# Where attention's values, the normalised x and the first branch sum are prepared in a one-core encoder block

## The chip, the cores and the metric

One core of a Trainium2 chip runs the whole program. The metric is the device time of one execution in microseconds (us); three executions of the kernel before the change give 1327.68 us (median; 1327.3 to 1328.23).

## What is computed

The reference is one layer (1024 tokens, width 1024): a mixer with two branches (chunked attention with 8 heads, and a spatial gating unit, SGU), gates on both branches, an output product, then a SwiGLU feed-forward part. The lines that this change touches:

```python
xn = rmsnorm(h, norm_mix[l])
proj = xn @ w_in[l]                      # q, k, v, u, vs, gate_logits
att = chunked_rel_attention(q, k, v, att_rel_bias[l])
sgu = spatial_gating(gelu(u), gelu(vs), ...)
br_att = att @ w_br_att[l]
br_sgu = sgu @ w_br_sgu[l]
gates = sigmoid(gate_logits + b_gate[l])
merged = gates[:, :, 0] * br_att + gates[:, :, 1] * br_sgu
h = h + merged @ w_out[l]
```

## The kernel before, in words

Everything lies transposed: 128 features on the partitions, 1024 tokens along the free axis in two halves of 512. An fp32 product is made of three TensorE passes: each operand is split into a high part (a cast on ScalarE) and a low part (source minus high part, on VectorE or GpSimd), and high x high, high x low and low x high are added in PSUM. So each operand costs one ACT cast and one DVE or POOL subtraction. There is no scheduler: the order of the Python statements is the order on each engine, and each engine works through its own list in order.

The stages that matter here, in order:

- **Attention** (`scores`, `exponents`, `turn`, `values`, `put_values`, loop over 64 steps of one head and 128 queries). `put_values` writes the outputs into `att[0..3]`, one tile for each pair of heads. Behind the loop, at line 676, all four are split into `attT` (line 156 is the common `split`), half by half.
- **Attention's branch products** `bw[0, 0..7]`, 24 matmuls each (`dense`, line 195, which calls `half_unit`, line 168): 12 for the first half of the tokens, 12 for the second, each half over the four blocks of `attT`. `begin` loads and splits the weights of the next products ahead (lines 123 and 125: hi on ACT, lo on POOL).
- **SGU values** (`gate_values`): `vs` is projected, put through gelu and normalised on DVE (lines 717 and 718).
- **Mixings** (`mix_positions(g)`, four groups, placed behind `bw[0, 4]`, `bw[0, 5]` and `bw[0, 6]`): 16 small matmuls (line 754), then on DVE lines 758 and 760, then the split into `sgu` (hi on ACT, lo on POOL).
- **SGU's branch products** `bw[1, 0..7]`, again 24 matmuls each. Beside them `gate_operands` makes the right-hand sides of the gate products: it loads x again (line 820), normalises it in eight blocks `xn` (line 825, DVE, 1024 wide), splits blocks into `b11` and `b21` and differences into `t1` (line 806 casts on ACT; line 173 subtractions, by turns on DVE and POOL), and forms further differences in place (line 812, DVE). A generator is stepped once in so many matmuls, which sets the place of each of these statements.
- **Gate products** (`order_m`, `product_m`, `collect_m`, line 182 on PE): a seven-product scheme; `collect_m` adds results on DVE and multiplies gates in (line 967).

`early` holds the first gate of each branch, computed ahead; line 620 evacuates it. `branch_evac(b, 0)` multiplies a branch by it (line 792) and adds both branches (line 795, POOL). The SP queue issues all loads, in the order of the statements. The pool `late` has 6 slots; the first three weight pairs of `vs` hold them until the last `vs` product, and then `xn0..5` take them.

Of the kernel before, what the change touches and what calls it, by code (L numbers as in the profile page):

```python
# [16 lines left out]
P = 128  # L17
# [31 lines left out]
def encoder_block(ctx: ExitStack, tc: tile.TileContext, xT, w_in, w_v, w_vs, w_att, w_sgu, w_out,  # L49
# [137 lines left out]
    def late_ops(keep, n=None):  # L187

        while len(pending) > keep and n != 0:
            if next(pending[0], 0) == 0:  # L190
                pending.pop(0)
            elif n is not None:
                n -= 1

    def dense(u, rhs, evac):

# [432 lines left out]
    with tc.tile_pool(name="apool", bufs=2) as apool:  # L629
        for n in range(2):  # L630
            load_bias(n)
            fill_bias(n)
        filler = chain(project_pair(1), project_u(0), project_pair(2), project_u(1), project_pair(3),
                       project_u(2), project_u(3), dense(gw[0], xg, early_gate(0)))
        state["due"] = 0
        turning = turn_queries(0, 1)
        for i in range(len(steps) + 2):
            if i % (2 * NT) == 0 and i < len(steps):
                j = i // (2 * NT)
                if j == PAIRS - 1:  # L640
                    late_ops(0)
                att.append(slot(f"att{j}", pool=more if j in (1, 2) else slots))
            share = SHARES[j][i % 2] if i < len(steps) - 2 else (4, 4)
            if i < len(steps):
                if i % (2 * NT) == 4 and j + 1 < PAIRS:
                    load_bias(2 * j + 2)
                scores(i)
                if i % (2 * NT) == 2 * NT - 2 and j + 1 < PAIRS:
                    load_bias(2 * j + 3)
# [12 lines left out]
            if i % (2 * NT) == NT + 1 and j + 1 < PAIRS:  # L662
                turning = turn_queries(j + 1, 0)
            elif i and i % (2 * NT) == 0 and i < len(steps):
                turning = turn_queries(j, 1)
            take(turning, 1)
            split_some()
            if i >= 2:
                values(i - 2)
        put_values(len(steps) - 1)  # L670
        attT = [two_slots(f"attT{j}") for j in range(PAIRS)]
        for s in halves:
            for j in range(PAIRS):
                split([x[:, s] for x in attT[j]], att[j][:, s], nc.gpsimd if j == 2 and s is halves[0] else nc.vector)
            drain(filler)
            late_ops(0)
            state["due"] = None
            if s is halves[0]:
                split_to(units.index(bw[0, 0]) + 2)
    late = mixer.enter_context(tc.tile_pool(name="late", bufs=6))  # L680

# [102 lines left out]
    def branch_evac(b, j):  # L784
        def evac(half, s, ps):
            if j % 2 == 0:
                branch[b, half].append(slot(f"br{b}_{half}_{j}", (P, 2, HALF)))
            dst = of_branch(b, half, j)
            if j:
                nc.scalar.copy(dst, ps)  # L790
            else:
                nc.vector.tensor_tensor(out=dst, in0=ps, in1=early[b][:, s], op=OP.mult)
                if b:
                    sum_ = of_branch(0, half, 0)
                    nc.gpsimd.tensor_tensor(out=sum_, in0=sum_, in1=dst, op=OP.add)
        return evac

    right_m, xn, low_m = {}, [], []
# [1 line left out]
    def at(k, half):  # L800
        return xn[k][half] if k == KB - 1 else xn[k][:, halves[half]]
# [9 lines left out]
    def minus(dst, a, b):  # L811
        nc.vector.tensor_tensor(out=dst, in0=a, in1=b, op=OP.subtract)

    def gate_operands():


        raw, tiles = [], None
        for k in range(KB):
            raw.append(slot(f"xn{k}", pool=late if k < 6 else more))
            nc.sync.dma_start(raw[k], xT[k * P:(k + 1) * P, :])  # L820

        def norm(k, s):
            last = k == KB - 1
            dst = tmp("xn7")[:, :] if last and s == halves[1] else raw[k][:, s]
            nc.vector.scalar_tensor_tensor(dst, raw[k][:, s], g_mix[:, k:k + 1], rstd[:, s], op0=OP.mult, op1=OP.mult)
            return dst

        xn.append(norm(0, slice(0, S)))
        yield 1
        for k in range(KB):  # L830
            if k + 2 < KB:
                xn.append(norm(k + 1, slice(0, S)))
                yield 1
            elif k + 2 == KB:
                xn.append([norm(k + 1, s) for s in halves])
                yield 1
            name = "b11" if k < 4 else "b21"
            if k % 2 == 0:
                tiles = [slot(f"{name}{x}{k}", (P, 2, HALF), F32R) for x in "hl"]
            put_m(name, k, at(k, 0), tiles, k % 2, nc.gpsimd if k % 2 else nc.vector)  # L840
            yield 1
        for k in range(4):
            if k % 2 == 0:
                tiles = [slot(f"t1{x}{k}", (P, 2, HALF), F32R) for x in "hl"]
            minus(at(k, 0), at(k, 1), at(k, 0))
            put_m("t1", k, at(k, 0), tiles, k % 2, nc.gpsimd if k % 2 else nc.vector)
            yield 1
        put_low(low_m)
        for k in range(4):
            minus(at(k, 0), at(4 + k, 1), at(k, 0))  # L850
            yield 1
            if k == 3:
                t4 = tmp("t4")
                minus(t4, at(7, 0), at(k, 0))
                xn[7][0] = t4
            else:
                minus(at(4 + k, 0), at(4 + k, 0), at(k, 0))
            yield 1
            minus(at(k, 1), at(4 + k, 1), at(k, 1))
            yield 1  # L860

    def other_operands_m():

# [19 lines left out]
    for j in range(KB):  # L883
        if j == 1:
            for n, _ in enumerate(dense(gw[1], xg, early_gate(1))):
                if n % 12 == 11:
                    split_to(units.index(vsw[n // 12]) + 1)
        for n, _ in enumerate(dense(bw[0, j], attT, branch_evac(0, j))):
            if n % 4 == 3:
                next(ending, 0)  # L890
        if j == 1:
            ending = gate_values()
            next(ending)
        for g in {4: (0,), 5: (1,), 6: (2, 3)}.get(j, ()):
            mix_positions(g)
            if g == GROUPS - 1:
                ending = gate_operands()
    banks.close()
    ps_f = ctx.enter_context(tc.tile_pool(name="ps_f", bufs=6, space=PSUM))
    psum.update(wide=None, dense=[(ps_f, "dense", 6)] * 6 + [(ps_d, "dense", 2)] * 2, n=-1)  # L900
# [57 lines left out]
    def collect_m(i):  # L958
# [23 lines left out]
        elif p == "2":  # L982
# [2 lines left out]
            yield 1  # L985
            gate(0, x, x)
            yield 1
            op(nc.gpsimd, of_branch(0, 0, j), x, of_branch(0, 0, j), OP.mult)
        elif p == "6":
            e["g"] = tmp(f"gb{j}")  # L990
            op(vector, e["g"], e["c2"], e["s"], OP.add)
# [687 lines left out]
```

## Time and profile before

| | us |
|---|---|
| median of three executions | 1327.68 (1327.3 to 1328.23) |
| the profiled execution | 1328.8 |
| its span, first to last instruction | 1327.1 |
| PE busy in it | 1304.7 (98%) |
| DVE busy | 941.0 (71%) |
| ACT busy | 570.4 (43%) |
| POOL busy | 423.4 (32%) |
| mean granted TensorE clock | 0.997 of full speed |

The page gives the busy time of each engine, the span in 40 slices, and the chain of work that ended last. A timeline row reads: start, length, engine, line, operation, output<-inputs, shapes, count; in brackets, the idle time of the engine just before and what ended it. Rows of several instructions are merged (x3), and instructions of one engine overlap a little, so starts, not lengths, give the pace. A row of a waiting list reads: engine and line, what it waited for, total us, how often, the longest.

### The profile page before, as it was taken

What the parts mean: (1) busy time and instruction counts of PE and PEld (TensorE: products, weight loads), DVE (VectorE), ACT (ScalarE), POOL (GpSimd) and SP (SyncE); (2) the same over time, 40 slices, a digit from 0 to 9 for tenths busy, and PEclk for the clock granted to TensorE, in tenths of its full rate; (3) what the DMA queues carried; (4) which work ended last, traced back from release to release, by engine and by line L of the source; (5) the groups of instructions that cost most, each with busy time, mean ns of one, the idle gap of its engine ahead of it and who ended that gap; (6) DMA issues with size and microseconds to landing.
All of it is one profiled execution on the core that took longest, in us unless ns stands there. A gap on an engine that the chain in (4) does not pass through costs nothing.

```text
span 1327.1 us, 17498 instructions
## 1 busy us (share of the span) xinstructions
PE 1304.7 (98%) x6290; PEld 1084.4 (82%) x6290; DVE 941.0 (71%) x1510; ACT 570.4 (43%) x1056; POOL 423.4 (32%) x343
## 2 busy tenths in 40 slices
PE   9999999999998999999999999999999999999997
PEld 7888888878886877888888888888888887888887
DVE  6256877871769778677767487878888857757455
ACT  7346666663334534444444034434444433212044
POOL 2525444324448355530000121221222222424232
PEclk9999999999999999999999999999999999999998
DMA  6001000103041211159883666666676669787723
GB/s 254 28 17 41 21 37 25 37 17 104 17 159 41 64 59 61 47 185 346 320 323 125 209 226 201 251 230 227 206 250 222 233 199 339 256 286 220 230 56 128
DMA packets 77879, 208.79 MB, mean 157 GB/s; under 512 B 8544, under 2 KB 12128, under 8 KB 77792
## 3 DMA queue, kind: packets, MB, share of 16 engines
q1 hardware_dynamic: 77792, 207.67, 45.4%
q8 instruction: 50, 0.82, 0.2%
q14 instruction: 37, 0.30, 0.1%
HBM read 140.01 MB, written 67.63 MB: 156 GB/s over the span
## 4 chain that ended last, share of the span: by engine, by line
PE 61%; DVE 1%; DMA 1%; issue 0%; ACT 0%; POOL 0%; DVEq 0%; ACTq 0%; POOLq 0%
PE c L182 44%; PE wo L1218 7%; PE mc L182 5%; PE last L168 3%; PE mp L182 2%; DMA g<-g_dram 1%; DVE mergedlo L782 0%; PE bc L277 0%; ACT wm_hi L155 0%; PE ss L1596 0%; DVE h_all L1606 0%; PE ss L1595 0%; DVE br L967 0%; PE ss L271 0%; DVE wg L932 0%
## 5 line engine op out<-in xcount | busy, mean ns | idle before, releaser
L1194 POOL TENSOR_TENSOR w_lo<-s,w_hi 128x512 fp32r<-128x512 f32 x54 | 78.1, 1452 | 318.2 <-ACT w_hi L1188 308.9
L182 PE MATMUL c<-t,g 128*128 128x512 f32 x432 | 103.8, 390 | 0.0
L182 PEld LDWEIGHTS c<-t,g 128*128 128x128 f32 x432 | 80.7, 188 | 18.4 <-DMA g<-g_dram 1.1
L1526 DVE TENSOR_TENSOR h_all<-h_all,c 128x512 f32<-128x512 f32 x72 | 49.0, 685 | 53.6 <-PE c L182 52.7
L182 PE MATMUL c<-b,g 128*128 128x512 f32 x324 | 78.5, 389 | 0.3 <-DMA g<-g_dram 0.3
L182 PEld LDWEIGHTS c<-b,g 128*128 128x128 f32 x324 | 60.7, 188 | 13.4 <-issue 0.7
L505 ACT ACTIVATE p<-p,low 128x640 f32<-128x640 f32 (+4 forms) x64 | 44.6, 697 | 58.5 <-DVE low L497 58.3
L1188 ACT CAST w_hi<-s 128x512 fp32r<-128x512 f32 x72 | 44.3, 619 | 41.7 <-DVE s L1150 38.0
L1490 ACT CAST t<-stage 128x512 fp32r<-128x512 f32 x36 | 22.2, 622 | 71.8 <-DVE stage L1487 66.4
L1365 ACT ACTIVATE g<-g 128x512 f32<-128x512 f32 x22 | 13.9, 633 | 86.2 <-DVE g L1364 80.0
L156 POOL TENSOR_TENSOR wm_lo<-wg,wm_hi 128x512 fp32r<-128x512 f32 x21 | 30.7, 1462 | 63.5 <-ACT wm_hi L155 55.7
L1218 PE MATMUL wo<-mergedhi,wo_hi 128*128 128x512 f32 x128 | 50.0, 391 | 0.0
L1218 PE MATMUL wo<-mergedhi,wo_lo 128*128 128x512 f32 x128 | 49.8, 389 | 0.0
L1218 PE MATMUL wo<-mergedlo,wo_hi 128*128 128x512 f32 x128 | 49.8, 389 | 0.0
L497 DVE CUSTOM_DVE_ANT_0 p<-s,bias 128x640 f32<-128x640 f32 (+4 forms) x64 | 41.7, 651 | 10.8 <-PE s L493 8.9
L261 POOL TENSOR_TENSOR rms_y<-rms_a,minus_half 128x4 f32<-128x4 f32 (+2 forms) x6 | 6.1, 1014 | 135.4 <-DVE rms_a L256 135.4
L173 POOL TENSOR_TENSOR t<-stage,t 128x512 fp32r<-128x512 f32 x18 | 26.8, 1492 | 59.6 <-ACT t L1490 55.2
L1254 ACT CAST gw<-fo 128x384 fp32r<-128x384 f32 x60 | 30.5, 510 | 34.4 <-DMA fo<-in_w_ffn_out 19.2
L523 DVE TENSOR_TENSOR ptl<-t,pth 128x640 fp32r<-128x640 f32 (+4 forms) x64 | 41.6, 651 | 4.5 <-ACT pth L522 4.3
L168 PE MATMUL last<-act_hi,fo 128*128 128x256 f32 (+1 forms) x192 | 43.8, 320 | 0.0
L507 DVE TENSOR_SCALAR p<-p,inv 128x640 f32<-128x640 f32 (+4 forms) x64 | 39.6, 619 | 2.3
L1238 DVE TENSOR_TENSOR gw<-fo,gw 128x384 fp32r<-128x384 f32 x60 | 40.2, 675 | 0.1
(428 smaller groups left out, 4242.3 us busy)
## 6 DMA issues: line engine op xcount, KB each, us to landing
g_dram<-gw SPq DMA_DIRECT2D x84, 384.0 KB, 2.7
g<-g_dram SPq DMA_DIRECT2D x84, 384.0 KB, 3.6
f_dram<-fw SPq DMA_DIRECT2D x28, 512.0 KB, 4.2
act_dram<-u SPq DMA_DIRECT2D x44, 256.0 KB, 2.6
stage<-act_dram SPq DMA_DIRECT2D x22, 512.0 KB, 7.3
fg<-in_w_ffn_in SPq DMA_DIRECT2D x18, 512.0 KB, 4.8
fu<-in_w_ffn_in SPq DMA_DIRECT2D x18, 512.0 KB, 4.1
fo<-in_w_ffn_out SPq DMA_DIRECT2D x24, 384.0 KB, 4.8
```

The lines of the kernel that those rows point to most:

```text
L156: (lo_engine or nc.gpsimd).tensor_tensor(out=lo, in0=src, in1=hi.bitcast(F32), op=OP.subtract)
L168: nc.tensor.matmul(ps, w, x[:, s], start=k == 0 and i == 0, stop=k == kc - 1 and i == 2)
L182: nc.tensor.matmul(ps, w[:, ws], x, start=first and k == 0 and n == 0, stop=k == last and n == 2, skip_group_check=True)
L497: nc.vector.tensor_tensor_reduce(out=p[:, :w].rearrange("p (a c) -> p a c", a=parts), in0=ps[:, :parts, :c], in1=bias.rearrange("p (a c) - ...
L505: nc.scalar.activation(e["p"], e["p"], AF.Exp, bias=e["low"], scale=-1.0, accum_out=e["tot"])
L507: nc.vector.tensor_scalar(e["p"], e["p"], e["inv"], None, op0=OP.mult)
L523: nc.vector.tensor_tensor(out=lo[:, :w], in0=ps[:, :w], in1=hi[:, :w].bitcast(F32), op=OP.subtract)
L1188: nc.scalar.copy(hi, src)
L1194: nc.gpsimd.tensor_tensor(out=lo, in0=src, in1=hi.bitcast(F32), op=OP.subtract)
L1218: nc.tensor.matmul(banks_w[j, half], w, x, start=k == 0 and n == 0, stop=k == KB - 1 and n == 2, skip_group_check=True)
L1238: nc.vector.tensor_tensor(out=t[:, width:2 * width], in0=src, in1=t[:, :width].bitcast(F32), op=OP.subtract)
L1526: nc.vector.tensor_tensor(out=dst, in0=dst, in1=banks_g[name, r], op=OP.add)
```

## The change

Five edits:

1. The split of `att` moves into the attention loop (`split_att`): pair j is split in the last steps, once it is complete; the second halves of pairs 0 to 2 have their low part made on POOL, all else on DVE. The first branch product `bw[0, 0]` uses a new order, `dense_late`: both halves over the first three pairs, and the fourth pair of both halves last.
2. The loads of `xn0..5` are issued right behind `gate_values`, ahead of three weight loads; `xn6` and `xn7` behind the last mixing.
3. `xn0..5` are normalised two at a time, placed ahead of each of the three mixing places; the splits of `b11`, `b21` and `t1` follow behind them, with all low parts on DVE.
4. Two operations move from POOL to DVE: the sum of both branches' first blocks (two halves), and one gate product of `collect_m` for j = 1.
5. `begin(bw[0, j + 1])` is called ahead of the mixings.

```diff
+    def dense_late(u, rhs, evac):
+
+        begin(u)
+        tiles = [dense_ps(f"{u['name']}_{half}") for half in range(2)]
+        late_ops(0)
+        last = len(rhs) - 1
+        for k, half in [(k, half) for half in range(2) for k in range(last)] + [(last, 0), (last, 1)]:
+            for i, (w, x) in enumerate(passes(u, k, rhs[k])):
+                nc.tensor.matmul(tiles[half], w, x[:, halves[half]], start=k == 0 and i == 0,
+                                 stop=k == last and i == 2, skip_group_check=True)
+                yield
...
+        def split_att(j, of=range(2)):
+
+            if j == len(attT):
+                attT.append(two_slots(f"attT{j}"))
+            for half in of:
+                s = halves[half]
+                split([x[:, s] for x in attT[j]], att[j][:, s], nc.gpsimd if j < 3 and half else nc.vector)
+
...
+            if i >= len(steps) - 1:
+                split_att(i - len(steps) + 1)
         put_values(len(steps) - 1)
-        attT = [two_slots(f"attT{j}") for j in range(PAIRS)]
-        for s in halves:
-            for j in range(PAIRS):
-                split([x[:, s] for x in attT[j]], att[j][:, s], nc.gpsimd if j == 2 and s is halves[0] else nc.vector)
+        for half in range(2):
+            split_att(PAIRS - 1, (half,))
...
-                    nc.gpsimd.tensor_tensor(out=sum_, in0=sum_, in1=dst, op=OP.add)
+                    nc.vector.tensor_tensor(out=sum_, in0=sum_, in1=dst, op=OP.add)
...
-        xn.append(norm(0, slice(0, S)))
+        def put_plain(ks):
+            for k in ks:
+                name = "b11" if k < 4 else "b21"
+                if k % 2 == 0:
+                    tiles[:] = [slot(f"{name}{x}{k}", (P, 2, HALF), F32R) for x in "hl"]
+                put_m(name, k, at(k, 0), tiles, k % 2)
+                yield 1
+
+        tiles = []
+        for k in range(6):
+            xn.append(norm(k, slice(0, S)))
+            yield 1
+        yield from put_plain(range(6))
...
-            put_m(name, k, at(k, 0), tiles, k % 2, nc.gpsimd if k % 2 else nc.vector)
...
-            put_m("t1", k, at(k, 0), tiles, k % 2, nc.gpsimd if k % 2 else nc.vector)
...
-        for n, _ in enumerate(dense(bw[0, j], attT, branch_evac(0, j))):
-            if n % 4 == 3:
+        for n, _ in enumerate((dense if j else dense_late)(bw[0, j], attT, branch_evac(0, j))):
+            if n % 4 == 3 and j < 3 or n % 8 == 3 and j == 7:
                 next(ending, 0)
         if j == 1:
             ending = gate_values()
             next(ending)
+            for k in range(6):
+                load_xn(k)
+        if 3 < j < 7:
+            begin(bw[0, j + 1])
         for g in {4: (0,), 5: (1,), 6: (2, 3)}.get(j, ()):
             mix_positions(g)
             if g == GROUPS - 1:
-                ending = gate_operands()
+                load_xn(6)
+                load_xn(7)
+        if j == 2:
+            drain(ending)
+            ending = gate_operands()
+        take(ending, {3: 2, 4: 2, 5: 2}.get(j, 0))
...
-            op(nc.gpsimd, of_branch(0, 0, j), x, of_branch(0, 0, j), OP.mult)
+            op(vector if j == 1 else nc.gpsimd, of_branch(0, 0, j), x, of_branch(0, 0, j), OP.mult)
```

How the instructions move, at three places. **DVE at the end of attention** (`ptl` are the transposed probabilities' low parts, `att3` the last pair, `attT0..3` the split pairs, `early0` the early gate). Before:

```order
L523 TENSOR_TENSOR ptl63_3255<-t63_3250,pth61_3195 128x512
L573 TENSOR_TENSOR att3_2616<-o60_3204,low62_3273 64x256
L573 TENSOR_TENSOR att3_2616<-o61_3242,low63_3292 64x256
L156 TENSOR_TENSOR attT0_lo_3296<-att0_642,attT0_hi_3295 128x512
L156 TENSOR_TENSOR attT1_lo_3298<-att1_1275,attT1_hi_3297 128x512
L156 TENSOR_TENSOR attT3_lo_3302<-att3_2616,attT3_hi_3301 128x512
L620 TENSOR_TENSOR early0_3237<-wg0_1_3239,rstd_337 128x512
```

and now:

```order
L156 TENSOR_TENSOR attT0_lo_3247<-att0_642,attT0_hi_3246 128x512
L539 TENSOR_TENSOR ptl63_3261<-t63_3256,pth61_3195 128x512
L156 TENSOR_TENSOR attT1_lo_3280<-att1_1275,attT1_hi_3279 128x512
L589 TENSOR_TENSOR att3_2616<-o60_3204,low62_3285 64x256
L156 TENSOR_TENSOR attT2_lo_3305<-att2_1934,attT2_hi_3304 128x512
L589 TENSOR_TENSOR att3_2616<-o61_3242,low63_3310 64x256
L156 TENSOR_TENSOR attT3_lo_3314<-att3_2616,attT3_hi_3313 128x512
L636 TENSOR_TENSOR early0_3237<-wg0_1_3239,rstd_337 128x512
```

Behind the early gate stood four more splits (pairs 0 to 3 of the second half); now one does, that of pair 3.

**DVE around the first mixing** (`mixed` is a mixing's result, `xn0..` are the normalised blocks). Before:

```order
L718 SCALAR_TENSOR_TENSOR vs3_3491<-vs3_3491,lnr_3493,rows_3334 128x512
L758 TENSOR_TENSOR mixed_3959<-mix0_3950,mix_3336 128x512
L760 SCALAR_TENSOR_TENSOR mixed_3959<-mixed_3959,gu0_1210 128x512
L758 TENSOR_TENSOR mixed_3964<-mix0_3950,mix_3336 128x512
L760 SCALAR_TENSOR_TENSOR mixed_3964<-mixed_3964,gu0_1210 128x512
L758 TENSOR_TENSOR mixed_4014<-mix1_4005,mix_3336 128x512
```

and now:

```order
L744 SCALAR_TENSOR_TENSOR vs3_3491<-vs3_3491,lnr_3493,rows_3334 128x512
L852 SCALAR_TENSOR_TENSOR xn0_3827<-xn0_3827,vec_83,rstd_337 128x1024
L852 SCALAR_TENSOR_TENSOR xn1_3829<-xn1_3829,vec_83,rstd_337 128x1024
L784 TENSOR_TENSOR mixed_3975<-mix0_3966,mix_3336 128x512
L786 SCALAR_TENSOR_TENSOR mixed_3975<-mixed_3975,gu0_1210 128x512
L784 TENSOR_TENSOR mixed_3980<-mix0_3966,mix_3336 128x512
L786 SCALAR_TENSOR_TENSOR mixed_3980<-mixed_3980,gu0_1210 128x512
L852 SCALAR_TENSOR_TENSOR xn2_3831<-xn2_3831,vec_83,rstd_337 128x1024
L852 SCALAR_TENSOR_TENSOR xn3_3833<-xn3_3833,vec_83,rstd_337 128x1024
L784 TENSOR_TENSOR mixed_4032<-mix1_4023,mix_3336 128x512
```

Two normalisations stand ahead of each mixing's evacuation; before, all eight came behind the last of them.

**POOL beside SGU's branch products** (`wb1_n` are those products' weights). Before:

```order
L156 TENSOR_TENSOR sgu3_lo_4082<-mixed_4097,sgu3_hi_4081 128x512
L125 TENSOR_TENSOR wb1_1_lo_4157<-wb1_1_raw_4102,wb1_1_hi_4156 128x512
L173 TENSOR_TENSOR b11l0_4136<-xn1_4111,b11h0_4135 128x512
L795 TENSOR_TENSOR br0_0_0_3356<-br0_0_0_3356,br1_0_0_4185 128x512
L125 TENSOR_TENSOR wb1_2_lo_4205<-wb1_2_raw_4165,wb1_2_hi_4204 128x512
L795 TENSOR_TENSOR br0_1_0_3375<-br0_1_0_3375,br1_1_0_4208 128x512
L173 TENSOR_TENSOR b11l2_4175<-xn3_4115,b11h2_4174 128x512
L125 TENSOR_TENSOR wb1_3_lo_4251<-wb1_3_raw_4211,wb1_3_hi_4250 128x512
L173 TENSOR_TENSOR b21l4_4221<-xn5_4119,b21h4_4220 128x512
```

and now:

```order
L156 TENSOR_TENSOR sgu3_lo_4102<-mixed_4117,sgu3_hi_4101 128x512
L125 TENSOR_TENSOR wb1_1_lo_4163<-wb1_1_raw_4078,wb1_1_hi_4162 128x512
L125 TENSOR_TENSOR wb1_2_lo_4212<-wb1_2_raw_4171,wb1_2_hi_4211 128x512
L125 TENSOR_TENSOR wb1_3_lo_4263<-wb1_3_raw_4218,wb1_3_hi_4262 128x512
L125 TENSOR_TENSOR wb1_4_lo_4305<-wb1_4_raw_4267,wb1_4_hi_4304 128x512
L125 TENSOR_TENSOR wb1_5_lo_4346<-wb1_5_raw_4310,wb1_5_hi_4345 128x512
```

POOL makes the weights' low parts alone; eight operations of the other kinds went to DVE.

## Rows read from the trace of the kernel before

**Rows 1.** Waits of PE: line, waited for, us in total, times, longest.

```profile
PE wb L168 <- POOL wb_lo L125: 3.3, 3, 2.1
PE mc L182 <- DVE gd L967: 2.0, 2, 1.1
...
PE wb L168 <- DVE attT_lo L156: 1.6, 1, 1.6
...
PE mc L182 <- POOL wm_lo L156: 1.0, 2, 0.6
```

**Rows 2.** Stages: length, busy PE PEld DVE ACT POOL, clock, DMA share, GB/s.

```profile
290.00:300.00 10.00, 8.24 (x35) 5.86 (x35) 8.34 (x10) 8.11 (x13) 3.99 (x2) 1.00 0.15 41
376.00:400.00 24.00, 24.00 (x140) 21.08 (x139) 12.27 (x17) 9.26 (x16) 14.71 (x10) 1.00 0.55 208
400.00:449.00 49.00, 45.23 (x195) 35.94 (x194) 44.96 (x36) 20.05 (x37) 32.34 (x19) 1.00 0.19 59
449.00:512.00 63.00, 60.05 (x260) 48.18 (x260) 49.16 (x64) 31.92 (x57) 27.32 (x20) 1.00 0.16 51
...
590.00:690.00 100.00, 100.00 (x454) 82.95 (x454) 69.11 (x118) 42.94 (x75) 2.03 (x2) 1.00 0.93 348
```

**Rows 3.** Timeline of PE: first matmul of `bw[0, 0]`, first one behind it.

```profile
291.71 0.40 PE L168 MATMUL wb<-attT_hi,wb_hi 128*128 128x512 f32 x1
...
299.84 0.39 PE L168 MATMUL wg<-xh,wg_hi 128*128 128x512 f32 x1
```

**Rows 4.** Chain of waits, output product's first half: start, length, count.

```profile
586.36 54.40 PE wo L1218 x240
```

**Rows 5.** Timelines of DVE, ACT and POOL at the end of attention.

```profile
294.90 4.07 DVE L156 TENSOR_TENSOR attT_lo<-att,attT_hi 128x512 fp32r<-128x512 f32 x4
...
292.81 1.05 ACT L123 CAST wg_hi<-wg_raw 128x1024 fp32r<-128x1024 f32 x1
...
293.99 2.63 POOL L125 TENSOR_TENSOR wg_lo<-wg_raw,wg_hi 128x1024 fp32r<-128x1024 f32 x1 [0.16 <-ACT wg_hi L123]
```

**Rows 6.** Timeline of PE: SGU's first branch matmul, first matmul of the gates.

```profile
399.91 0.39 PE L168 MATMUL wb<-sgu_hi,wb_hi 128*128 128x512 f32 x1
...
448.59 0.39 PE L182 MATMUL mp<-b11h,wm_hi 128*128 128x512 f32 x1
```

**Rows 7.** Timelines of POOL, DVE and ACT beside them.

```profile
419.98 3.44 POOL L173 TENSOR_TENSOR b21l<-xn,b21h 128x512 fp32r<-128x512 f32 x2
...
399.03 5.74 DVE L825 SCALAR_TENSOR_TENSOR xn<-xn,vec,rstd 128x1024 f32<-128x1024 f32 x3
427.58 1.78 DVE L173 TENSOR_TENSOR t1l<-xn,t1h 128x512 fp32r<-128x512 f32 x1
...
424.01 1.23 ACT L806 CAST t1h<-xn 128x512 fp32r<-128x512 f32 x2 [4.00 <-DVE xn L812]
```

**Rows 8.** The tile `xn`, 340 to 420 us: min/median/max ns, first and last start.

```profile
L825 DVE SCALAR_TENSOR_TENSOR xn<-xn,vec,rstd x9: 1273/2296/2319, 399.0 to 418.8; 128x1024 f32<-128x1024 f32 x7, 128x512 f32<-128x512 f32 x2
...
DMA to landing us min/median/max: 3.7/7.4/10.6
```

**Rows 9.** Timelines of DVE and POOL at the mixings.

```profile
378.39 0.69 DVE L758 TENSOR_TENSOR mixed<-mix,mix 128x512 f32<-128x512 f32 x1 [2.68 <-PE mix L754]
...
398.03 1.07 DVE L760 SCALAR_TENSOR_TENSOR mixed<-mixed,gu 128x512 f32<-128x512 f32 x1
...
395.09 7.39 POOL L156 TENSOR_TENSOR sgu_lo<-mixed,sgu_hi 128x512 fp32r<-128x512 f32 x4 [2.23 <-ACT sgu_hi L155]
```

**Rows 10.** Timelines of DVE, POOL and PE in the gate products.

```profile
461.15 1.88 DVE L173 TENSOR_TENSOR t4b22l<-xn,t4b22h 128x512 fp32r<-128x512 f32 x3
465.73 0.69 DVE L967 TENSOR_TENSOR gd<-mc,br 128x512 f32<-128x512 f32 x1 [2.70 <-POOL br L967]
...
464.40 1.30 POOL L967 TENSOR_TENSOR br<-ga,br 128x512 f32<-128x512 f32 x1
...
468.85 0.47 PE L182 MATMUL mc<-t4b22h,wm_hi 128*128 128x512 f32 x1 [1.06 <-DVE gd L967]
```

More of the change, by code (lines that the diff above doesn't have):

```diff
@@ L193, in late_ops @@
                 n -= 1
+    def dense_late(u, rhs, evac):
[8 more added lines that the diff above has]
+                yield
+            if k == last:
+                if half:
+                    split_soon(units.index(u) + 3)
+                evac(half, halves[half], tiles[half])
     def dense(u, rhs, evac):
@@ L636, in encoder_block @@
         turning = turn_queries(0, 1)
+        attT = []
+        def split_att(j, of=range(2)):
[4 more added lines that the diff above has]
+                split([x[:, s] for x in attT[j]], att[j][:, s], nc.gpsimd if j < 3 and half else nc.vector)
         for i in range(len(steps) + 2):
@@ L677, in encoder_block @@
             state["due"] = None
-            if s is halves[0]:
+            if half == 0:
                 split_to(units.index(bw[0, 0]) + 2)
@@ L812, in minus, with load_xn @@
         nc.vector.tensor_tensor(out=dst, in0=a, in1=b, op=OP.subtract)
+    raw = []
+    def load_xn(k):
+        raw.append(slot(f"xn{k}", pool=late if k < 6 else more))
+        nc.sync.dma_start(raw[k], xT[k * P:(k + 1) * P, :])
     def gate_operands():
[L817 to L820, printed above, removed]
         def norm(k, s):
@@ L826, in norm @@
             return dst
-        xn.append(norm(0, slice(0, S)))
-        yield 1
[L830 to L839, printed above, removed]
-            put_m(name, k, at(k, 0), tiles, k % 2, nc.gpsimd if k % 2 else nc.vector)
[L841 to L845, printed above, removed]
-            put_m("t1", k, at(k, 0), tiles, k % 2, nc.gpsimd if k % 2 else nc.vector)
-            yield 1
+        def put_plain(ks):
[10 more added lines that the diff above has]
+        yield from put_plain(range(6))
+        for k in range(5):
+            if k < 4:
+                minus(at(k, 0), at(k, 1), at(k, 0))
+            if k % 2 == 1:
+                tiles[:] = [slot(f"t1{x}{k}", (P, 2, HALF), F32R) for x in "hl"]
+            if k:
+                put_m("t1", k - 1, at(k - 1, 0), tiles, (k - 1) % 2)
+            yield 1
+        while len(raw) < KB:
+            yield 1
+        xn.append(norm(6, slice(0, S)))
+        yield 1
+        xn.append([norm(7, s) for s in halves])
+        yield 1
+        plain = put_plain((6, 7))
         put_low(low_m)
@@ L860, in gate_operands @@
             yield 1
+            if k < 2:
+                next(plain)
+                yield 1
+        put_low(low_m)
     def other_operands_m():
```

## The prediction

> **What bounds the kernel.** I read the waits of PE first: PE is busy 98% of the span, so time can be won only where it stands still. Its list is short [rows 1]: SGU's branch products wait three times for a weight's low part on POOL (3.3 us), attention's first branch product once for `attT_lo` on DVE (1.6), and the gate products for `gd` on DVE (2.0) and for weights on POOL (1.0). The busy times by stage put these stops where the diff is: PE is idle 1.76 us of 290 to 300, nothing in 376 to 400, 3.77 in 400 to 449 and 2.95 in 449 to 512 [rows 2]. A stop costs a little more than its idle time (the restart), so I count by pace: in the chain of waits 240 matmuls of 512 columns take 54.40 us, 0.227 each, hence 5.44 for one branch product of 24 [rows 4].
>
> - Attention's first branch product runs from 291.71 to 299.84 [rows 3]: 8.13, so 2.69 above pace.
> - SGU's eight run from 399.91 to 448.59 [rows 6]: 48.68 against 192 x 0.227 = 43.52, so 5.16 above pace.
> - The gate products lose 2.95 idle plus restarts.
>
> Next I read why these parts come late, on DVE, ACT and POOL. An SBUF subtraction of 512 columns costs DVE 0.60 at pace (three in 1.88, one being 0.69 long [rows 10]) and POOL 1.30 alone [rows 10]. Where both run such operations, they take turns: POOL then needs 1.72 each (3.44 for two), DVE 1.78 [rows 7]. A normalisation of a block takes 1.27 at best and 2.30 at the median [rows 8], for the same reason. From 400 to 449 DVE is busy 44.96 of 49 us and POOL 32.34 [rows 2]: they hold each other up, the weights' low parts stand in POOL's list between others, and ACT waits up to 4.00 us for DVE with the next weight's cast behind it [rows 7].
>
> **The change, part by part.** I lay times out on the clock of the profile before; all that runs earlier shifts together.
>
> *Split of `attT`.* Before, PE stops because the second half's first `attT_lo` is the fourth split on DVE behind the loop, and POOL's 2.63 us for the gate weight holds DVE up: the four from 294.90 take 4.07 where four at pace take 2.4 [rows 5]. Now pairs 0 to 2 are split inside the loop, and 18 matmuls (4.1 us) need none of pair 3. Its first half comes early enough. Its second half has its cast behind the gate weight's cast (292.81 + 1.05 [rows 5]), so about 294.0 at the earliest once that weight's cast moves up a little; by then POOL has begun the gate weight and keeps DVE out until about 296.2, so the low part is ready near 296.8. PE wants it 22 matmuls in, at 296.7. I book 2.4 of the 2.69 (2.0 to 2.69). Moved into the loop: six casts and six subtractions, in steps where DVE's and ACT's next work waits for PE anyway; without that cover they would cost at most their own length on POOL, 1.30 once.
>
> *Copies of x.* Six copies of 512 KB now stand ahead of three weight loads in SP's queue. Their slots come free with the last `vs` product, and three branch products (16.3 us) lie between that and the first mixing; before, eight copies landed within 10.6 us [rows 8]. So they are there in time, and the weight behind them, first needed after those three products, too. Cost 0.
>
> *Normalising between mixings.* DVE is idle half of 376 to 400 (busy 12.27 of 24.00 [rows 2]), waiting for PE 2.68 us before the first evacuation [rows 9]. Six operations of 1.27 are 7.6 us, plus up to 1.30 whenever POOL is in its `sgu_lo` or a weight. Placing them one by one, the evacuations of the first two groups end by about 388.7, the last two normalisations by 393.3, and the last evacuation at 399.8 instead of 399.10 (398.03 + 1.07 [rows 9]). `sgu_lo` of group 3, first half, then ends at 401.1 (before: about 400.6, three quarters of the 7.39 from 395.09 [rows 9]); PE wants it 10 matmuls behind 399.91, at 402.2. Spare 1.1: cost 0. If the copies or POOL are later than that, each further us is one on PE.
>
> *POOL left to the weights.* This is the largest term. From 400 on POOL has only seven weight subtractions of 1.30, and loses eight other operations. DVE gains those eight (8 x 0.60 = 4.8) and has lost 7.6 of normalising ahead. The tightest product is the fourth: its cast stands on ACT behind the fourth `t1` cast, which needs the fifteenth DVE operation after 399.8. Four POOL operations get in between, at 1.75 for each pair in turns (between 1.72 and 1.78 [rows 7]), and eleven run alone: 11 x 0.60 + 4 x 1.75 = 13.6, so DVE is through at 413.4. Two casts of 0.62 [rows 7] and one 1.30 give 415.9; PE wants that low part at 399.91 + 72 x 0.227 + 0.45 = 416.7. The spare is 0.8, more if the two of the fifteen that read PSUM overlap with POOL. The second weight has about 1.0 to spare by the same count, the others more. I book 4.6 of the 5.16 (3.0 to 5.16).
>
> Here POOL's 1.72 in turns is 1.30 plus 0.42: DVE's 0.69 is not held to its end. The Trainium skill (SBUF — State Buffer, "SBUF: two separate sides") says that the engine that begins first keeps the shared port pair for the whole instruction. By that rule a pair in turns would take 0.69 + 1.30 = 1.99, four pairs 1.0 more, and PE would wait 0.2 us at the fourth product (1319.9 in the end); this trace's 1.72 does not agree.
>
> *Gate products.* DVE's first `gd` waits 2.70 us for POOL's `br` [rows 10]; that multiplication now stands on DVE directly ahead of it (+0.60) and POOL loses 1.30. DVE restarts near 463.0 instead of 465.73, but two POOL weights that were hidden in that idle time now fall between its SBUF operations, 2.6 us in all. So the second `gd` comes about 0.7 to 1.0 earlier, and the stop at 468.85 (1.06 [rows 10]) shrinks to near 0.3; the weight behind it moves up by as much. I book 1.0 of the 2.95 (0 to 2.0). The later stops follow PE through their own chain and stay.
>
> *The sum of both branches* on DVE is among the eight. *`begin` ahead of the mixings* moves no cast and no subtraction: the end of each branch product already asks for as many. Cost 0.
>
> Sum: 2.4 + 4.6 + 1.0 = 8.0 us. Against the profiled execution, 1328.8 (span 1327.1 and 1.7 around it), that gives 1320.8; it lies 1.1 above the median of the runs, 1327.68, so I predict **1319.7**.
>
> **The rivals.**
> 1. *DVE is the new bound beside SGU's products.* The fifteen operations come 3.3 us later than laid out (POOL wins more turns, or the mixings end later), and the fourth weight stops PE for 2.5: 1322.2. For it: the spare is 0.8 on a chain of some 16 us. Against: the DVE and POOL work of the stage shrinks.
> 2. *The `attT` stop stays*, because POOL's 2.63 still stands ahead of pair 3's last split: 2.0 less, 1321.7. For it: the wait I found at 296.7. Against: only one subtraction is behind that lock, not four.
> 3. *The time is given back at the transfers.* From 590 to 690 the DMA engines are 93% busy [rows 2]; if they set the pace there, PE arrives 8 us early and waits. With three quarters given back: 1325.7. Against: PE has no stop there, and each transfer is released by an engine that is itself earlier.
> 4. *Slower: DVE's list is stopped by the copies of x.* The normalisations stand ahead of the evacuations; if a copy lands late, evacuation, `sgu` and PE wait in a row. It decides from the point where the last evacuation slips by more than the 1.1 spare; to lose more than the 8.0 won it must slip by 9. At 12 us: 1319.7 + 10.9 = 1330.6. Against: 16.3 us of cover for copies that took 10.6 at most.
>
> That the change doesn't do what it says holds for `begin` alone and is priced at 0.
>
> **How the numbers follow.** Forecast 0.63, rival 1 0.17, rival 2 0.07, rival 3 0.08, rival 4 0.05. About 0.2%, 2.66 us, is what a measurement of this kernel can tell from no change. The forecast and rivals 1 and 2 are faster by more: 0.87. Rival 3 is within it: 0.08. Rival 4: 0.05. The bounds of the terms reach from 2.69 + 5.16 + 2.0 = 9.85 won (1317.8) to 5.0 (1322.7); with a little for stops that go unasked and for rival 1's tail the range is 1317.2 to 1323.6, which leaves out rivals 3 and 4.
>
> **What would show it.** Right: no wait of `wb` for `wb_lo` or `wb_hi` over 0.5 us, attention's first product in under 5.9 us, SGU's eight in 43.5 to 44.2, DVE's wait for POOL's `br` gone, one stop for `gd` left under 0.6. Wrong: a wait of SGU's products for `sgu_lo` or for the fourth weight, normalisations of 2.3 us that push an evacuation past 400, or a new stop after 512.

## The result, and the profile after

The changed kernel takes 1319.32 us (median of four runs, 1318.67 to 1319.5) against 1327.65 of the kernel before beside it: ratio 0.9934, 95% interval 0.9922 to 0.9945, or 8.3 us less. Forecast were 1319.7, between 1317.2 and 1323.6.

The profiled execution took 1319.5, its span 1317.8; in it PE is busy 1302.7 us (99%), DVE 943.6, ACT 570.8, POOL 414.4, at a mean granted clock of 0.997. The three parts of the prediction, each from its first matmul to the first matmul behind it:

| us | before | after |
|---|---|---|
| attention's first branch product | 8.13 | 5.44 |
| SGU's eight branch products | 48.68 | 43.89 |
| gate products | 137.61 | 136.55 |

They won 2.69, 4.79 and 1.06, in sum 8.54. The two profiled spans differ by 9.3, about 0.8 more. That lies behind the gate, where the code is the same: from there to the last matmul it is 734.1 before and 733.2 after, and it was 732.7 to 734.7 in the profiles below, so it is the spread of single executions (attention's first product began 0.15 later, which takes a little off again). The medians are 8.3 apart.

The waits of PE after (line, waited for, us in total, times, longest) answer to [rows 1]:

```profile
PE mc L182 <- POOL wm_lo L156: 1.0, 2, 0.6
PE mc L182 <- DVE gd L1015: 0.9, 1, 0.9
```

The waits of `wb` for POOL's `wb_lo` (3.3) and for `attT_lo` (1.6) are gone from the list, and of two waits for `gd` one is left. The stages, with the columns of [rows 2]:

```profile
290.00:300.00 10.00, 10.00 (x48) 8.36 (x47) 6.16 (x7) 6.47 (x9) 5.39 (x3) 1.00 0.50 141
376.00:400.00 24.00, 24.00 (x132) 20.77 (x131) 22.48 (x22) 10.54 (x19) 19.52 (x11) 1.00 0.26 77
400.00:449.00 49.00, 48.92 (x217) 40.17 (x216) 36.87 (x44) 23.72 (x45) 15.85 (x10) 1.00 0.20 60
449.00:512.00 63.00, 61.07 (x265) 49.05 (x264) 53.64 (x67) 29.13 (x52) 30.32 (x20) 1.00 0.18 55
590.00:690.00 100.00, 100.00 (x454) 82.98 (x454) 72.52 (x124) 43.30 (x76) 2.02 (x2) 1.00 0.87 323
```

PE (the first busy time) is idle nowhere in 290 to 300 and for 0.08 us in 400 to 449, where it was 3.77. DVE went from 12.27 to 22.48 in the stretch of the mixings and from 44.96 to 36.87 behind it; POOL from 32.34 to 15.85. In the last row PE is full although the transfers are nearly as dense as before (a share of 0.87 against 0.93): nothing is given back there. The timeline of PE (start, length, engine, line, operation) gives the borders of the two parts, as [rows 3] and [rows 6] did:

```profile
291.86 0.39 PE L203 MATMUL wb<-attT_hi,wb_hi 128*128 128x512 f32 x1
...
297.30 0.39 PE L168 MATMUL wg<-xh,wg_hi 128*128 128x512 f32 x1
...
397.38 0.39 PE L168 MATMUL wb<-sgu_hi,wb_hi 128*128 128x512 f32 x1
...
441.27 0.39 PE L182 MATMUL mp<-b11h,wm_hi 128*128 128x512 f32 x1
```

The second group starts 2.53 us earlier than before; times of the two profiles are compared below by that shift.

### The profile page after: what moved, and what is told of

Its sections match the earlier page's. It is cut to its first block, busy times and chain, and to the rows that moved or that the text cites. A ratio compares the mean times of both kernels' runs of the same rounds, so it can differ in the third digit from the quotient of the medians.

```text
span 1317.8 us, 17501 instructions
## 1 busy us (share of the span) xinstructions
PE 1302.7 (99%) x6290; PEld 1085.6 (82%) x6290; DVE 943.6 (72%) x1517; ACT 570.8 (43%) x1056; POOL 414.4 (31%) x336
## 4 chain that ended last, share of the span: by engine, by line
PE 62%; DVE 1%; issue 0%; ACT 0%; POOL 0%; DVEq 0%; ACTq 0%; POOLq 0%
PE c L182 45%; PE wo L1266 7%; PE mc L182 5%; PE last L168 3%; PE mp L182 2%; DVE mergedlo L808 0%; PE bc L293 0%; ACT wm_hi L155 0%; PE ss L1644 0%; DVE h_all L1654 0%; PE ss L1643 0%; DVE br L1015 0%; PE ss L287 0%; DVE wg L980 0%; POOL wm_lo L156 0%
## 5 line engine op out<-in xcount | busy, mean ns | idle before, releaser
L513 DVE CUSTOM_DVE_ANT_0 p<-s,bias 128x640 f32<-128x640 f32 (+4 forms) x64 | 41.7, 652 | 10.8 <-PE s L509 9.1
```

Source lines behind the costliest of these rows:

```text
L513: nc.vector.tensor_tensor_reduce(out=p[:, :w].rearrange("p (a c) -> p a c", a=parts), in0=ps[:, :parts, :c], in1=bias.rearrange("p (a c) - ...
```

## The experiments

All ran beside the kernel before on the same chip, with five or more executions. Their medians blur by about 1 us, partly at the start of the program: in one profile below attention's first branch product begins at 294.5, in others at 291.5 to 292.5, ahead of any edit. So each experiment is judged by the length of its stage in its profile too. The stretch between attention's first product and SGU's first is 100.05 to 100.09 us long in every profile. "First", "SGU" and "gate" are the three stages of the table above.

| kernel | median | ratio to before | first | SGU | gate |
|---|---|---|---|---|---|
| after, again | 1319.30 | 0.9932 [0.9919, 0.9945] | 5.44 | 43.89 | 136.42 |
| 1 plain order | 1318.99 | 0.9937 [0.9923, 0.995] | 5.46 | 43.95 | 136.62 |
| 2 late split of `attT` | 1322.17 | 0.9959 [0.9946, 0.9971] | 8.18 | 43.89 | 136.69 |
| 3 POOL shares again | 1320.02 | 0.9943 [0.993, 0.9955] | 5.44 | 44.22 | 136.91 |
| 4 before, POOL relieved | 1328.57 | 1.0006 [0.9997, 1.0015] | 8.17 | 50.52 | 137.50 |
| 5 gate operation on POOL | 1321.36 | 0.9945 [0.9932, 0.9957] | 5.46 | 43.89 | 137.44 |
| 6 no early `begin` | 1319.25 | 0.9931 [0.9918, 0.9944] | 5.46 | 43.90 | 136.41 |
| 7 gate weight on DVE | 1320.01 | 0.9934 [0.992, 0.9947] | 5.44 | 43.90 | 136.11 |
| 8 banks freed first | 1321.63 | 0.9946 [0.9933, 0.9958] | 5.46 | 43.89 | 136.99 |
| 9 three normalised early | 1320.67 | 0.9946 [0.9933, 0.9958] | 5.46 | 44.79 | 136.75 |
| 10 none early | 1319.64 | 0.9932 [0.9918, 0.9947] | 5.46 | 44.04 | 136.54 |
| 11 seven and eight | 1320.02 | 0.9936 [0.9923, 0.9949] | 5.46 | 43.90 | 136.33 |

The kernel before beside numbers 1 to 4 took 1327.92, beside 5, 7, 8 and 9 1328.52, beside the others 1328.11. The run of the unchanged kernel after:

> The kernel after itself, unchanged, beside the others of this call, so that differences below 1 us are read on the same chip. Every theory expects 0.993 to 0.994 of the time before, SGU's eight products 43.7 us and the gate products 136.3 to 136.5 us.

It gave 43.89 and 136.42, so stage lengths repeat to 0.15. (The lengths in the expectations run to the start of a stage's last matmul and are 0.2 shorter than the table's, which run to the first matmul behind it.)

**The split of `attT` (1 and 2).** Number 1 takes the plain order of the product:

```diff
-        for n, _ in enumerate((dense if j else dense_late)(bw[0, j], attT, branch_evac(0, j))):
+        for n, _ in enumerate(dense(bw[0, j], attT, branch_evac(0, j))):
```

> The kernel after, with attention's first branch product in the plain order (first half all four pairs, then second half) in place of the late order. Theory (the early split of pairs 0 to 2 is the whole gain): the plain order wants pair 3's second low part at the same 22nd matmul as the late order, and pair 3's first low part at the 10th, some 2.3 us in, when it has been ready for about 1 us; so nothing changes: the product stays at 5.4 to 5.6 us and the kernel at 1319.3, within 0.3. Rival (the late order is needed): pair 3's first half stops PE, the product takes 6 to 7.5 us and the kernel 1320 to 1321.4.

5.46 against 5.44: the late order does nothing here; the theory holds. Number 2 also puts the split back behind the loop:

```diff
-            if i >= len(steps) - 1:
-                split_att(i - len(steps) + 1)
...
-        for half in range(2):
-            split_att(PAIRS - 1, (half,))
+        attT = [two_slots(f"attT{j}") for j in range(PAIRS)]
+        for half, s in enumerate(halves):
+            for j in range(PAIRS):
+                split([x[:, s] for x in attT[j]], att[j][:, s], nc.gpsimd if j == 2 and s is halves[0] else nc.vector)
```

> The kernel after, with attT split behind the loop as before and the plain order; everything else as after. Theory (the three savings are independent and add): the 2.7 us of attention's first branch product come back, 8.1 in place of 5.4, and nothing behind it changes: 1322.0, between 1321.5 and 1322.5. Rival (time won there is partly absorbed later, at the stops of SGU and of the gate): under 1.5 us come back, below 1320.9.

The wait of the kernel before is back, and the 2.7 us with it; SGU and gate stay as they were, so this saving adds to the others. Its waits of PE:

```profile
PE wb L168 <- DVE attT_lo L156: 1.6, 1, 1.6
```

**What frees SGU's products (3, 4, 9 and 10).** Number 3 gives POOL its eight operations back, number 4 takes them from it in the kernel before:

```diff
-                put_m(name, k, at(k, 0), tiles, k % 2)
+                put_m(name, k, at(k, 0), tiles, k % 2, nc.gpsimd if k % 2 else nc.vector)
...
-                    nc.vector.tensor_tensor(out=sum_, in0=sum_, in1=dst, op=OP.add)
+                    nc.gpsimd.tensor_tensor(out=sum_, in0=sum_, in1=dst, op=OP.add)
```

> The kernel after, with POOL doing its old share beside SGU's branch products (every second low part of the operands and both sums of branches, eight operations), and the normalisations still between the mixings. Theory (POOL's list is what held the weights up): waits for weights come back, 1.5 to 4 us of the 4.7, 1320.8 to 1323.3. Rival (the normalisations moved ahead are what freed the stage): the waits stay away, at most 0.5 us, below 1319.9. If the eight products take more than 48.7 us, moving the normalisations alone would be harmful, which neither expects.

> The kernel before, with only these eight operations moved from POOL to DVE; normalisations, attT and gate as before. Theory (POOL's list held the weights up): SGU's eight products go from 48.7 to about 44 to 46 us, the kernel to 1323 to 1325. Rival (the normalisations had to leave first): DVE gets 4.8 us more to do in a stage where it was busy 92%, ACT's casts of weights stand behind casts that wait for DVE, and the products keep a loss of 4 us or more: 1327 or slower.

Both answers go against the theory. With POOL sharing, SGU's products take 0.33 us more, one wait of 0.4. With POOL relieved in the kernel before, they take 1.84 us more than in the kernel before itself, and the whole comes out the same. (About 3.0 us of the 50.52 are a fall of TensorE's clock, see the last section; without it the stage would take some 47.5, about 1 less than before, an estimate.) The waits of PE in number 3, and then in number 4:

```profile
PE wb L168 <- POOL wb_lo L125: 0.4, 1, 0.4
```

```profile
PE wb L168 <- POOL wb_lo L125: 2.8, 2, 2.2
...
PE wb L168 <- ACT wb_hi L123: 0.5, 1, 0.5
```

Number 4 does end one stop, the longest of the kernel before. There the third weight's cast was done at 408.8, but on POOL the sum of both branches stood ahead of its low part and waited for `br` on DVE. ACT, POOL and PE of the kernel before:

```profile
408.15 0.61 ACT L123 CAST wb_hi<-wb_raw 128x512 fp32r<-128x512 f32 x1
...
410.51 1.67 POOL L795 TENSOR_TENSOR br<-br,br 128x512 f32<-128x512 f32 x1 [1.77 <-DVE br L792]
412.14 2.25 POOL L125 TENSOR_TENSOR wb_lo<-wb_raw,wb_hi 128x512 fp32r<-128x512 f32 x1
...
414.44 0.50 PE L168 MATMUL wb<-sgu_hi,wb_lo 128*128 128x512 f32 x1 [2.12 <-POOL wb_lo L125]
```

In number 4 this low part begins at 408.88, and PE doesn't wait for it: so much of the theory holds. But the fifth weight, which stopped PE for 0.44 and 0.62 before, now stops it for 0.50 and 2.23. POOL holds nothing but weights there, and the fifth `wb_lo` comes late all the same: its cast came late, and the subtraction itself took 2.89 us in place of 1.30, beside a DVE that never paused.

```profile
423.29 2.89 POOL L125 TENSOR_TENSOR wb_lo<-wb_raw,wb_hi 128x512 fp32r<-128x512 f32 x1 [7.27 <-ACT wb_hi L123]
```

So the question was whether it is the early normalisations that count. Numbers 9 and 10 take three and all six of them back:

```diff
-        take(ending, {3: 2, 4: 2, 5: 2}.get(j, 0))
+        take(ending, {3: 1, 4: 1, 5: 1}.get(j, 0))
```

> The kernel after, with three normalisations between the mixings in place of six; the other three stand on DVE behind the last evacuation; all low parts and both sums still on DVE. Theory (DVE's list up to the fourth weight's cast is the bound, with next to no spare left): three operations of 1.27 to 2.3 us more in that list, 3.8 to 6.9 us back, so 1323 to 1326. Rival (what counts is that POOL holds only weights): at most 0.5 us back, below 1319.8.

> The kernel after, with none of the normalisations between the mixings: all six stand on DVE behind the last evacuation; all low parts and both sums still on DVE. With three early, SGU's eight products took 44.6 us against 43.7, though DVE had 6.9 us more in its list: some 5 to 6 us of it were spare time and collisions that went elsewhere. Theory (DVE's list is the bound once that is used up): from here each further normalisation costs its own length, 1.3 to 2.3 us, so 3.8 to 6.9 us more for three: products of 48 to 51 us, the kernel 1323.5 to 1327. Rival (POOL holds only weights, which is what keeps PE fed): products of 44 to 45.5 us, at most 1321.5.

(Number 10 has no `take` at all.) The theory of DVE's list fails in both. The rival's figures fail in number 9 and come out, near enough, in number 10, but its reason, a POOL that holds only weights, is the one that number 3 speaks against. Three late cost 0.9, six late only 0.15, although in number 10 DVE has no rest from 396.8 on: its timeline, start and length first.

```profile
396.79 10.22 DVE L852 SCALAR_TENSOR_TENSOR xn<-xn,vec,rstd 128x1024 f32<-128x1024 f32 x5
...
408.25 1.28 DVE L852 SCALAR_TENSOR_TENSOR xn<-xn,vec,rstd 128x1024 f32<-128x1024 f32 x1
...
411.16 2.48 DVE L173 TENSOR_TENSOR b11l<-xn,b11h 128x512 fp32r<-128x512 f32 x4
...
418.99 4.67 DVE L852 SCALAR_TENSOR_TENSOR xn<-xn,vec,rstd 128x1024 f32<-128x1024 f32 x3
```

What numbers 3 and 10 have in common with the kernel after, and number 4 has not, is the order of the list: all six normalisations first, then the casts of the plain blocks, then `t1` with each cast one step behind its subtraction, and blocks 6 and 7 (three normalisations, the last row above, and two low parts) behind `t1`. What this order does is seen on ACT. The waits of ACT from 399 to 430, in the kernel before:

```profile
ACT b21h L806 <- DVE xn L825: 6.8, 4, 2.8
ACT t1h L806 <- DVE xn L812: 4.9, 2, 4.0
ACT b11h L806 <- DVE xn L825: 4.6, 3, 1.9
```

and in number 10:

```profile
ACT br L816 <- PE wb L168: 6.7, 4, 2.3
ACT wb_hi L123 <- PE wb L168: 3.3, 1, 3.3
ACT t1h L832 <- DVE xn L838: 3.1, 2, 2.8
```

In the old order normalisation and cast of the same block alternate, so seven casts wait for a DVE normalisation, 11.4 us in all (10.8 in number 4), and the weights' casts, woven among them, wait too. In number 10, with the new order, no cast waits for one: ACT is early and mostly waits for PE. With the casts of `t1` ACT's waits for `xn` in this stretch are 16.3 us before and 13.0 in number 4, against 6.9 in number 3, 5.0 after, 3.5 in number 9 and 3.1 in number 10. Number 4's timeline of ACT shows the price at the fifth weight; the number in brackets is the idle time before.

```profile
417.13 0.62 ACT L806 CAST b21h<-xn 128x512 fp32r<-128x512 f32 x1 [2.54 <-DVE xn L825]
...
420.87 0.62 ACT L806 CAST t1h<-xn 128x512 fp32r<-128x512 f32 x1 [1.36 <-DVE xn L812]
422.07 0.62 ACT L806 CAST t1h<-xn 128x512 fp32r<-128x512 f32 x1 [0.58 <-DVE xn L812]
422.60 0.61 ACT L123 CAST wb_hi<-wb_raw 128x512 fp32r<-128x512 f32 x1
```

The theory that remains: an SGU stop comes where a weight stands in an engine's list behind an operation that waits for DVE. In the kernel before this is a cast on ACT at three stops (0.59, 0.44 and 0.62 us) and the sum on POOL at the longest (2.12); a low part that POOL makes beside a busy DVE draws the stop out (number 4). The new order makes these waits fewer and shorter; on POOL too, for in number 3 the sums are back there and begin without idle time. POOL's relief is not needed (number 3) and does not suffice (number 4), each in the company that it was tried in; the early place of the normalisations is worth 0.15, no more than stages repeat to, beside the new order with POOL relieved (number 10).

What else number 4 lacks hardly counts: without the early `attT` (number 2), the early `begin` (6) or the gate edit (5) SGU still takes 43.9, and in the kernel before DVE stood idle ahead of no normalisation, so none waited for its copy of x. Still, the new order alone in the kernel before was not tried, nor its two halves apart (casts away from their normalisations, and blocks 6 and 7 behind `t1`); which half does more is open.

Why three late normalisations cost more than six is seen in the place of the fourth weight. In number 9 its cast stands behind a `t1` cast that waits for DVE, and its low part then takes 4.09 us beside DVE; PE stands still for 0.97. ACT and POOL there:

```profile
410.60 0.62 ACT L832 CAST t1h<-xn 128x512 fp32r<-128x512 f32 x1 [3.55 <-DVE xn L838]
411.12 0.61 ACT L123 CAST wb_hi<-wb_raw 128x512 fp32r<-128x512 f32 x1
...
411.81 4.09 POOL L125 TENSOR_TENSOR wb_lo<-wb_raw,wb_hi 128x512 fp32r<-128x512 f32 x1 [6.14 <-PE wb L168]
```

In number 10 the `t1` casts come so late that this weight's cast stands ahead of them, at 408.59, and its low part takes 1.40. No run moved this cast alone.

**The gate (5, 7, 8 and 11).** Number 5 undoes the gate edit:

```diff
-            op(vector if j == 1 else nc.gpsimd, of_branch(0, 0, j), x, of_branch(0, 0, j), OP.mult)
+            op(nc.gpsimd, of_branch(0, 0, j), x, of_branch(0, 0, j), OP.mult)
```

> The kernel after, with the one multiplication of the first gate column back on POOL. Theory (it is this multiplication, late on POOL, that held DVE's gd and with it PE): the stop for gd at the start of the gate products, 1.06 idle and 1.2 with its restart, returns: 1320.5, between 1320.2 and 1320.8. Rival (the gate's gain comes from an emptier DVE list at its start): no stop returns, within 0.3 of 1319.2.

Its waits of PE:

```profile
PE mc L182 <- DVE gd L1015: 2.0, 2, 1.0
```

Two waits for `gd` again, the gate 0.9 to 1.0 us longer: the theory holds, the term being 0.9 to 1.0 rather than the 1.2 expected. Numbers 7 and 8 go for two of the stops that are left:

```diff
-            split([x[:, c] for x in parts_m[i // 2]], src, nc.vector if p in "67" else None)
+            split([x[:, c] for x in parts_m[i // 2]], src, nc.vector if p in "67" or (p, j) == ("3", 1) else None)
```

> The kernel after, with the low part of the weight of the ninth gate product (form 3, column 1) on DVE in place of POOL: aimed at the wait of 0.6 us of PE for wm_lo near 463.4. Theory (POOL's list is the last to arrive, DVE has 0.7 us idle just behind): the stop and its restart, 0.75, go: 1318.5. Rival (the wait is handed on to the gd and the weight behind it): the same time as after, 1319.2, with a stop for gd or for wm_lo some products later.

```diff
+        earlier = pending[:]
+        if p in "73":
+            g = collect_m(i)
+            next(g)
+            pending.append(g)
-        for g in pending[:]:
+        for g in earlier:
...
-        g = collect_m(i)
-        if next(g, 0):
-            pending.append(g)
+        if p not in "73":
+            g = collect_m(i)
+            if next(g, 0):
+                pending.append(g)
```

> The kernel after, with the reading of a gate product's PSUM bank by DVE (forms 7 and 3) put ahead of the split of merged values that is due in the same step: aimed at PE's wait of 0.9 us for gd near 497.4. Theory (two splits of 1.4 and 1.8 us stand on DVE ahead of the addition that frees the bank): the stop and its restart, 1.1, go: 1318.1. Rival (the output projection behind needs the split values as early, or POOL's weights there are late as well): 1319.2, with a stop of about 1 us elsewhere.

PE's waits in number 7, then in number 8:

```profile
PE mc L182 <- DVE gd L1015: 0.9, 1, 0.9
...
PE mc L182 <- ACT wm_hi L155: 0.7, 1, 0.7
```

```profile
PE mc L182 <- POOL wm_lo L156: 1.6, 3, 0.6
```

In number 7 both waits for `wm_lo` are gone and one of 0.7 for the next weight's `wm_hi` has come: the gate is 0.3 to 0.45 shorter, so most of the wait is handed on, as the rival said, and a part is won. In number 8 the wait for `gd` is gone and a third wait for `wm_lo` of 0.6 has come, at 512: the gate is 0.4 to 0.6 longer. There the rival holds. Number 11 joins number 7 with the first place of number 8:

> The kernel after with the gate weight of the ninth product on DVE, and the bank of the 28th or so (form 7, column 3) freed ahead of the splits of merged values: the two edits tried singly, the second only at its first place. Singly the first made the gate products 0.45 us shorter (135.9 against 136.3), the second moved a stop of 1.1 us from 497 to 512, where it was 0.8. Theory (the gate's stops are one chain through DVE and ACT that hands a saved wait on): 0.4 to 0.8 us less than the kernel after, 1318.5. Rival (the stops are separate): 1.9 us less, 1317.4.

136.33 and 1320.02: nothing that can be told from the kernel after, so neither the 0.4 to 0.8 of the theory nor the 1.9 of the rival came. The waits of 0.7 for `wm_hi` and of 0.6 for `wm_lo` of the two single edits are both there. No version tried is ahead of the kernel after by more than the medians blur.

**Asking early for the weights (6).** `if 3 < j < 7` was left out.

> The kernel after, without the asking for the next weight ahead of the mixings: only the place of two copies of x in SP's queue changes, by one row. Prediction's term (0): the same time as the kernel after within 0.3, no wait for a weight in the products around the mixings. Rival (the early asking hides a weight behind the mixing): a wait of PE for wb_5 to wb_7 of 0.5 us or more appears.

No wait came, 43.90: the edit is worth nothing, as booked.

## Why the prediction was right, point by point

- *Split of `attT`*: booked 2.4, measured 2.69, the upper bound. The wait that I feared at the end of the product did not come. The timelines of DVE and POOL:

```profile
292.18 0.69 DVE L156 TENSOR_TENSOR attT_lo<-att,attT_hi 128x512 fp32r<-128x512 f32 x1 [0.74 <-ACT attT_hi L155]
...
293.65 2.52 DVE L156 TENSOR_TENSOR attT_lo<-att,attT_hi 128x512 fp32r<-128x512 f32 x1 [0.18 <-ACT attT_hi L155]
```

```profile
293.23 2.40 POOL L125 TENSOR_TENSOR wg_lo<-wg_raw,wg_hi 128x1024 fp32r<-128x1024 f32 x1 [1.53 <-ACT wg_hi L123]
```

 POOL did hold the last `attT_lo` up as I said (2.52 for 0.69), but the gate weight began at 293.23, not at 294, so the low part was there at 296.2, ahead of the 296.85 at which PE used it. The new order of the product, of which I had made 18 matmuls of cover, was not needed (number 1).
- *Copies of x and normalising between mixings*: booked 0, nothing stopped. The last evacuation ended at 396.95, which is 399.5 by the clock of before (I had 399.8).

```profile
395.88 1.07 DVE L786 SCALAR_TENSOR_TENSOR mixed<-mixed,gu 128x512 f32<-128x512 f32 x1
```

- *POOL left to the weights*: booked 4.6, measured 4.79. The number is right and the name is wrong in the main. My count of fifteen DVE operations up to the fourth `t1` cast ended at 413.4; the fourth subtraction ended at 410.8, which is 413.3 by the same clock. But I had counted in the new order, in which blocks 6 and 7 come later, without pricing that order as an edit, and put its worth down to POOL. The runs show that POOL's relief is worth 0.33 beside the rest. By itself it ends the longest stop, as I said, and the time is lost again at the fifth weight and by the clock (number 4). That the term came out so near is right as a count of all edits together, and luck as the price of this one. The rows told it: in [rows 7] ACT waits 4.00 us for DVE with a weight's cast behind it, and I read that as DVE and POOL in each other's way.
- *Where the spare of 0.8 went*: rival 1 has the right place. The fourth weight held PE 0.24 us over its pace, since its low part took 2.31 in place of the 1.30 that I counted; a normalisation on DVE had begun just ahead.

```profile
411.90 1.28 DVE L852 SCALAR_TENSOR_TENSOR xn<-xn,vec,rstd 128x1024 f32<-128x1024 f32 x1
```

```profile
412.03 2.31 POOL L125 TENSOR_TENSOR wb_lo<-wb_raw,wb_hi 128x512 fp32r<-128x512 f32 x1 [6.74 <-ACT wb_hi L123]
```

 I had weighed the Trainium skill's rule that the engine that begins first keeps the shared port pair for the whole instruction ("SBUF — State Buffer", "SBUF: two separate sides") and set it aside for the short pairs in turns. For this pair the trace nearly agrees: held to the end of the normalisation, 413.18, and 1.30 more would be 414.48, and POOL ended at 414.34. The 1.72 to 1.78 for a pair in turns, on which the count rests, is not the most that POOL can lose either: its subtraction took 2.89 in number 4 and 4.09 in number 9.
- *Gate products*: booked 1.0, measured 1.06 (0.9 to 1.0 by number 5). The split of it was off: the first `gd` wait did not shrink to 0.3 but went (0.17 over pace is left), and the weight behind it kept its 0.6. The wait of 0.9 for a later `gd` stayed, as said.

```profile
455.64 0.68 DVE L1015 TENSOR_TENSOR br<-ga,br 128x512 f32<-128x512 f32 x1
456.43 0.69 DVE L1015 TENSOR_TENSOR gd<-mc,br 128x512 f32<-128x512 f32 x1
...
459.65 0.68 DVE L1015 TENSOR_TENSOR gd<-mc,gd 128x512 f32<-128x512 f32 x1
```

 Against [rows 10] the 2.70 us of idle time ahead of `gd` are gone, and the second `gd` starts at 459.65 and is done at 460.33, just ahead of PE at 460.48.
- *The rivals*: rival 2 did not come (5.44); rival 3 did not (590 to 690 is full); rival 4 did not, since the copies of x landed within 8.0 us of their issue and the last evacuation slipped by 0.4 only. The sum, 8.0 booked against 8.5 in the stages and 8.3 in the medians, is off by the 0.3 of the first term and 0.2 of the second.

## What to carry to other kernels

When several edits meet in one stage, a count made with all of them in place gives the sum but not what each is worth: count again with each one undone before giving the gain a name. Where an in-order engine weaves two kinds of work, look at what its urgent operations stand behind; moving a cast a few steps away from the operation that feeds it can free a chain without making any operation shorter (seen here with other edits beside it, not alone). A stop of under 1 us in a stage whose engines all run close together can be handed to the next place, in whole or in part, when it is attacked alone (numbers 7 and 8).

## What the runs showed of the hardware

Number 4's profile has a fall of the granted clock that neither the kernel before nor the kernel after has there. PE stood for 0.50 us up to 423.3 and for 2.23 us up to 426.2. Its timeline around that, and its windows:

```profile
422.37 0.39 PE L168 MATMUL wb<-sgu_hi,wb_lo 128*128 128x512 f32 x1
423.26 0.50 PE L168 MATMUL wb<-sgu_hi,wb_hi 128*128 128x512 f32 x1 [0.50 <-ACT wb_hi L123]
...
426.23 0.79 PE L168 MATMUL wb<-sgu_hi,wb_lo 128*128 128x512 f32 x1 [2.23 <-POOL wb_lo L125]
...
427.24 0.63 PE L168 MATMUL wb<-sgu_lo,wb_hi 128*128 128x512 f32 x1
427.67 0.63 PE L168 MATMUL wb<-sgu_hi,wb_lo 128*128 128x512 f32 x1
```

```profile
424.00:428.00 4.00, 1.77 (x4) 1.49 (x5) 3.92 (x4) 2.32 (x5) 3.86 (x2) 0.68 0.19 50
428.00:432.00 4.00, 4.00 (x11) 3.02 (x11) 3.93 (x7) 0.59 (x1) 0.00 (x0) 0.50 0.25 81
432.00:436.00 4.00, 4.00 (x19) 3.30 (x18) 3.86 (x6) 1.10 (x2) 1.13 (x1) 0.97 0.00 0
```

Behind the second stop the matmuls start 0.43 us apart, not 0.227, at a granted clock of 0.50 (the level of 1.2 GHz), and near 432 the clock is back. One matmul at 0.36 more and 13 at about 0.2 more each are 3.0 us, more than the stop itself. That is why SGU's products take 50.5 us there, though its three stops with their restarts (0.85, 0.77 and 2.40) add up to 4.0 only, 1.0 less than in the kernel before. The kernel before had a longest wait of 2.1 [rows 1] and kept the clock at 1.00 [rows 2]; whether the stop that is 0.1 longer or the one of 0.50 just ahead of it makes the difference was not shown. Number 4's executions lie between 1326.47 and 1331.34, a wider spread than that of any other kernel here, at mean granted clocks of 0.994 (the profiled one) to 0.998. The kernel before has 0.996 or 0.997 in the 15 executions beside it. So this fall is probably not in every execution of number 4; only one was profiled.

The other thing is POOL's subtraction of 512 columns. It took 1.30 us alone [rows 10], but 2.31 (after), 2.89 (number 4), 3.51 (number 10) and 4.09 (number 9) where DVE went from one operation to the next without a pause. A list that leaves POOL only weights does not by itself make their low parts quick.
